# Forming the sums of the FFN's weights in DRAM by adding transfers

## The chip, the core and the metric

The kernel runs on one core of one Trainium2 chip. Its engines are TensorE (PE), VectorE (DVE), ScalarE (ACT) and GpSimd (POOL); SyncE (SP) issues transfers, and 16 DMA engines move them. Each engine takes its instructions in one fixed order. The metric is the device time of one execution in microseconds (us), the median of the runs.

## The reference

One decoder block on 1024 tokens of width 1024 in float32:

```
u    = rmsnorm(x, g1);  proj = u @ w_in          # queries, keys, values, mLSTM inputs, gates
ya   = sliding_window_attention(q, k, v, sinks) @ w_attn_branch      # 8 heads of 64, window 128
ym   = (rmsnorm(mlstm(...), gm) * sigmoid(mo)) @ w_mlstm_branch      # 4 heads, chunks of 128
x    = x + (sigmoid(ga) * ya + sigmoid(gm) * ym) @ w_out
f    = rmsnorm(x, g2)
x    = x + (silu(f @ w_ffn_gate) * (f @ w_ffn_up)) @ w_ffn_down      # inner width 2816
out  = rmsnorm(x, g3)
```

## The kernel before

Every float32 operand of a product is split into two parts, hi and lo, of a format that PE multiplies: ACT rounds hi, and DVE or POOL subtracts it for lo (`split`, line 71). A product is three matmuls, hi·hi, hi·lo and lo·hi. Weights come in blocks of 128 columns (`weights`, line 75).

The program has these stages. In the opening x and the first weights are loaded, and u is split. Since the norm of a token is a factor of its row, products with u start at once, and the factor 1/rms goes in when a bank of PSUM is emptied. That factor, `rstd1`, is made from sums of squares by a power on POOL (line 141); PE spreads it with an identity into rows (`rows_of`, line 146), ACT stores them as `Rt`, and DVE multiplies the queries with them as it empties the banks (line 229). Seven banks hold query products till then. Then come keys, values, the attention in 16 units (`attn_a`, `attn_b`, `attn_c`), in which POOL subtracts the lo part of each unit's queries (line 289) and scales the probabilities by 1/den (line 314), mixed with the convolution's projections, whose lo parts POOL makes as well; the mLSTM; the two branches' projections; and the output projection.

The FFN follows. It uses a product scheme with seven products in place of eight for a 2 by 2 arrangement of blocks (the indices 1 to 7 in `ORDER` and `DORD`). Four of the seven take a sum or difference of blocks of the weights x11, x12, x21, x22: 5 is x21 + x22, 6 is that + x11, 7 is x11 + x21, 3 is x12 + sum 6. Gate and up have 22 such sets of seven products (pair n, `product7`), 11 for gate and 11 for up. Before, SP loads the four blocks of a set (`load_pair`, line 791), and POOL forms the four sums in SBUF (line 813) ahead of the split (`prep`, line 805). The inner activations and their sums go to DRAM (`hd_`, `h_store`, line 867). Down reads them back by `dload` (line 959), with blocks of its weights, and POOL forms their sums (lines 987 to 995), with a copy on ACT for two of them, ahead of the split in `dprep`.

The program is written in one order and recorded; a scheduler then places each engine's instructions by its own estimate of when they can start. A written place is thus no fixed place: what depends on nothing can move to the front of its engine's order.

Of the kernel before, what the change touches and what calls it, by code (L numbers as in the profile page):

```python
# [15 lines left out]
P = 128  # L16
# [2 lines left out]
FF = 2816  # L19
KD = D // P  # L20
NF = FF // P
NT = S // P
HALF = 512
EPS = 1e-6
# [5 lines left out]


@with_exitstack
def hybrid_block(ctx, tc, xT, xt, par, g3row, cst, abias, w_fm, w_mv, w_br, w_o, w_gu, w_dn, out):
    nc = tc.nc
    V, A, G, T = nc.vector, nc.scalar, nc.gpsimd, nc.tensor

# [14 lines left out]
    def blk(name, dtype=F32, n=1024):  # L51
        return sb.tile([P, n], dtype, name=name, tag="blk", bufs=NB)
# [22 lines left out]
    def weights(src, nk, w=P):  # L75

        return weights_split(weights_load(src, nk * w), nk, w)
# [36 lines left out]
    def hs(h):  # L114
        return slice(h * HALF, (h + 1) * HALF)
# [517 lines left out]
    run(gai, 16)  # L633


    ph_a.close()
    lo_eng[0] = V
    ph_b = ExitStack()
# [22 lines left out]
            os_[h][p] = (pv2(hi), pv2(lo))  # L661
    o_ = lambda k, h: tuple(b[:, k % 2] for b in os_[h][k // 2])
    for j in range(KD):
        wt = weights(w_br[j], 4)
        A.activation(mg[j], mg[j], AF.Sigmoid)
        for h in range(2):
            ps = proj(wt, o_, 4, h)
            V.tensor_tensor(mg[j][:, hs(h)], ps, mg[j][:, hs(h)], ALU.mult)


    hs_ = [[None, None], [None, None]]
    for i in range(4):
# [14 lines left out]

    m = []
    for j in range(KD):
        wt = weights(w_fm[22 + j], KD)  # L690
# [12 lines left out]
        split(hi, lo, mg[j])  # L703
        m.append((hi, lo))
# [66 lines left out]
    def half(name, tag, bufs):  # L771
        return pC.tile([P, HALF], F32, name=name, tag=tag, bufs=bufs)
# [9 lines left out]


    ORDER = (1, 6, 5, 7, 2, 3, 4)
    NP2 = NF // 2
# [3 lines left out]
    raws, hl, sums = {}, {}, {}  # L789

    def load_pair(n):

        raws[n] = [x for i in range(2) for x in pair_raw(n, i)]

    def pair_raw(n, i):
        if n == 0 and i == 1:
            r = [half("wr", "ev", 6) for _ in range(2)]
            for k in range(2):
                nc.sync.dma_start(out=r[k], in_=w_gu[n, i, :, hs(k)])
            return r  # L800
        r = blk("wr2") if i else wp.tile([P, 1024], F32, name="wraw", tag="wraw", bufs=2)
        nc.sync.dma_start(out=r, in_=w_gu[n, i])
        return halves(r)

    def prep(g):
        n, i = SEQ[g]
        if n and i == 6 and n + 1 < 2 * NP2:
            load_pair(n + 1)
        x11, x12, x21, x22 = raws[n]

        def s_(k, a, b):
            sums[n, k] = half("s_", "ws", 5)
            G.tensor_tensor(sums[n, k], a, b, ALU.add)  # L813
        if i in (5, 6) and (n, 5) not in sums:
            s_(5, x21, x22)
        if i == 6:
            s_(6, sums[n, 5], x11)
        elif i == 7:
            s_(7, x11, x21)
        elif i == 3:  # L820
            s_(3, x12, sums[n, 6])
        src = {1: x11, 2: x12, 4: x22}
        hi = wp.tile([P, HALF], F32R, name="whi", tag="whi", bufs=5)
        lo = wp.tile([P, HALF], F32R, name="wlo", tag="wlo", bufs=5)
        split(hi, lo, src[i] if i in src else sums[n, i])
        hl[n, i] = (hi, lo)

    later = []
    for j in range(KD):
        wt = weights(w_o[j], KD)  # L830
        xr = wp.tile([P, 1024], F32, name="xr2", tag="wraw", bufs=2)
        nc.sync.dma_start(out=xr, in_=xT[j])
        xc = blk("xc")
        f = blk("f")
        F_.append(f)
        g = prm[:, C_G2 + j:C_G2 + j + 1]
        if j == KD - 1:
            load_pair(0)
            prep(0)
            prep(1)  # L840
        for h in range(2):
            ps = proj(wt, m_, KD, h)
            V.tensor_tensor(xc[:, hs(h)], ps, xr[:, hs(h)], ALU.add)
            A.activation(f[:, hs(h)], xc[:, hs(h)], AF.Copy, scale=g)
            later.append((xc, j, h))
            if len(later) > 1:
                to_tokens(*later.pop(0))
        if j % 2 == 1 and j < 6:
            f_even(j // 2)
        elif j == 6:  # L850
            f_split(1, 3, F_[6][:, 0:HALF])
# [81 lines left out]
            if i == 4 and s == 1:  # L933
                h_sums(n // 2, sg)

    load_pair(1)

    def f_rest(i, kt):
        (z11, z12), (z21, z22) = halves(F_[2 * kt]), halves(F_[2 * kt + 1])
# [9 lines left out]
    DORD = (1, 5, 2, 3, 6, 7, 4)  # L949
    NC_ = 7 * NP2  # L950
    LD, LP = 6, 4
    draw, dop, sT, dtm = {}, {}, {}, {}

    def t_at(p):
        if (p // 2) not in sT:
            sT[p // 2] = blk("sT")
        return halves(sT[p // 2])[p % 2]

    def dload(c):

        i, p = DORD[c // NP2], c % NP2
        t = blk("ld")
        draw[c] = t
        nc.sync.dma_start(out=t[:, 0:HALF], in_=hd_[i - 1, p])

        def ld(k, j, dst=None):
            dst = half("lz", "ev", 6) if dst is None else dst
            nc.sync.dma_start(out=dst, in_=w_dn[2 * p + k, :, hs(j)])
            return dst
        z = t[:, HALF:1024]  # L970
        if i in (1, 2, 3):
            ld(*{1: (0, 0), 2: (1, 0), 3: (1, 1)}[i], z)
        elif i == 5:
            dtm[c] = ld(0, 0), ld(0, 1)
        elif i == 7:
            dtm[c] = ld(1, 1), ld(0, 1)
        elif i == 6:
            dtm[c] = (ld(1, 1),)
        else:
            dtm[c] = (ld(1, 0),)  # L980

    def dprep(c):
        i, p = DORD[c // NP2], c % NP2
        t = draw.pop(c)
        z, tm = t[:, HALF:1024], dtm.pop(c, None)
        if i == 5:
            G.tensor_tensor(t_at(p), *tm, ALU.add)
            A.activation(z, t_at(p), AF.Copy)
        elif i == 6:
            G.tensor_tensor(t_at(p), tm[0], t_at(p), ALU.add)  # L990
            A.activation(z, t_at(p), AF.Copy)
        elif i == 7:
            G.tensor_tensor(z, *tm, ALU.add)
        elif i == 4:
            G.tensor_tensor(z, tm[0], t_at(p), ALU.add)
        hi, lo = blk("xzh", F32R), blk("xzl", F32R)
        split(hi, lo, t)
        dop[c] = hi, lo

    z11, z12 = halves(F_[6])  # L1000
# [2 lines left out]
        f_rest(6, kt)  # L1003
    prep(2)
    prep(3)
    rest = [(i, kt) for i in (7, 2, 3, 4) for kt in range(4)]
    for g, (n, i) in enumerate(SEQ):
        if g + LA < len(SEQ):
            prep(g + LA)
        product7(n, i)  # L1010
        if g == 0:
            to_tokens(*later.pop(0))
            V.tensor_tensor(rstd2, ss2[:, 0], ss2[:, 1], ALU.add)
            rstd_of(rstd2, rstd2, D, NT)
        if n == 2 * NP2 - 1 and i in (7, 2, 3):
            for c in {7: range(LP), 2: range(2), 3: range(2, LP)}[i]:
                (dload if i == 7 else dprep)(c)
        for _ in range(2):
            if rest:
                f_rest(*rest.pop(0))  # L1020
# [95 lines left out]
def _layout(i):  # L1116
# [30 lines left out]
    def cols(w):  # L1147
# [12 lines left out]
    w_br = np.concatenate([cols(wa), cols(a["w_mlstm_branch"][0])], axis=0)  # L1160
    w_o = cols(a["w_out"][0])

    w_gu = np.stack([cols(a[k][0]).reshape(NF // 2, 2, P, 4, 2, P).transpose(0, 1, 2, 4, 3, 5).reshape(NF // 2, 2, P, D)
                     for k in ("w_ffn_gate", "w_ffn_up")], axis=1).reshape(NF, 2, P, D)
    w_dn = a["w_ffn_down"][0].reshape(NF, P, D)
    return [xT, x.reshape(NT, P, D), par, np.tile(a["final_norm_g"][None, :], (P, 1)), cst, abias, w_fm, w_mv, w_br, w_o, w_gu, w_dn]


_NAMES = ["xT", "xt", "par", "g3row", "cst", "abias", "w_fm", "w_mv", "w_br", "w_o", "w_gu", "w_dn"]


# [15 lines left out]
```

## Time and profile before

| | us |
|---|---|
| median of 3 runs | 1335.22 (1332.36 to 1336.35) |
| the profiled execution | 1331.28 |
| its span, first to last instruction | 1329.5 |
| PE busy in the span | 1303.4 (98%) |
| DVE, ACT, POOL busy | 765.0, 572.7, 458.5 |
| moved by DMA | 143.13 MB, mean 108 GB/s |

The profiled execution is 1.8 us longer than its span and 3.9 us below the median. A busy time is the sum over an engine's instructions; matmuls overlap, so busy 98% means that PE hardly waits. The row of the granted clock in the page's slices is 9 (of tenths, 9 is 90% or more) in all but two of the 40 slices, where it is 8.

### The profile page before, as it was taken

Reading aid. Unit: us, or ns where it says so; the run is one execution under the profiler, and the core shown is the slowest. Engines: PE = TensorE matmul, PEld = TensorE weight load, DVE = VectorE, ACT = ScalarE, POOL = GpSimd, SP = SyncE. Lnnn points to the kernel's source line nnn. Section 1 sums busy time; section 2 is a strip of 40 time slices with the busy share of each in tenths; the row PEclk is TensorE's granted clock in tenths of the full one; section 3 lists DMA queues with packets and bytes.
Section 4 is the critical chain, followed back from the end, with each engine's and each line's share of the span. In section 5 each row is a group of like instructions: output and inputs, shape, how many; then the busy total and the mean of one; then the engine's idle time right before and its main releaser. Section 6 shows DMA issues by size and latency. Waiting matters only on the chain.

```text
span 1329.5 us, 16764 instructions
## 1 busy us (share of the span) xinstructions
PE 1303.4 (98%) x6090; PEld 1066.1 (80%) x6090; DVE 765.0 (58%) x1261; ACT 572.7 (43%) x1078; POOL 458.5 (34%) x374
## 2 busy tenths in 40 slices
PE   8999999999999999999989999999999999999986
PEld 6888998777888888888778888888888888888865
DVE  5369764565535444433587555555556564664796
ACT  6369974566213222224453333333233344565333
POOL 0245443211000000010266657556655725600470
PEclk9999999999999999999989999999999999999989
DMA  9111011101111111224323321323232249983761
GB/s 338 48 57 39 17 33 48 49 9 33 56 48 42 44 48 49 73 64 158 121 67 121 119 97 71 103 103 119 104 119 82 85 168 309 331 287 92 261 230 64
DMA packets 61860, 143.13 MB, mean 108 GB/s; under 512 B 6992, under 2 KB 7248, under 8 KB 61776
## 3 DMA queue, kind: packets, MB, share of 16 engines
q1 hardware_dynamic: 61776, 142.05, 31.7%
q8 instruction: 48, 0.79, 0.2%
q14 instruction: 36, 0.29, 0.1%
HBM read 113.45 MB, written 28.57 MB: 107 GB/s over the span
## 4 chain that ended last, share of the span: by engine, by line
PE 87%; DVE 7%; issue 2%; ACT 1%; DMA 1%; POOL 1%; SPq 0%; DVEq 0%; POOLq 0%; ACTq 0%
PE mm L108 8%; PE mm L110 7%; PE mm L109 7%; PE mm L856 6%; PE mm L857 6%; PE mm L855 6%; PE mb L856 5%; PE mb L857 5%; PE mb L855 5%; PE st L857 4%; PE st L855 4%; PE st L856 4%; PE mb L110 4%; PE mb L109 4%; PE mb L108 4%
## 5 line engine op out<-in xcount | busy, mean ns | idle before, releaser
L72 ACT ACTIVATE whi<-wraw 128x512 fp32r<-128x512 f32 (+1 forms) x144 | 89.3, 628 | 221.3 <-PE mb L109 99.8
L73 DVE TENSOR_TENSOR xzl<-ld,xzh 128x1024 fp32r<-128x1024 f32 x77 | 110.4, 1463 | 69.3 <-ACT xzh L72 62.0
L108 PE MATMUL mm<-uh,whi 128*128 128x512 f32 x352 | 140.0, 400 | 1.1 <-ACT whi L72 1.1
L110 PE MATMUL mm<-uh,wlo 128*128 128x512 f32 x352 | 139.0, 395 | 0.0
L109 PE MATMUL mm<-ul,whi 128*128 128x512 f32 x352 | 138.7, 395 | 0.0
L73 DVE TENSOR_TENSOR wlo<-wraw,whi 128x512 fp32r<-128x512 f32 (+1 forms) x116 | 88.6, 771 | 76.4 <-ACT whi L72 75.5
L72 ACT ACTIVATE xzh<-ld 128x1024 fp32r<-128x1024 f32 x77 | 79.7, 1056 | 58.5 <-DMA ld<-in_w_dn_dram 24.9
L857 PE MATMUL mb<-z,wlo 128*128 128x512 f32 x220 | 87.8, 399 | 1.8 <-DVE wlo L73 1.8
L856 PE MATMUL mb<-z,whi 128*128 128x512 f32 x220 | 87.7, 399 | 0.0
L855 PE MATMUL mb<-z,whi 128*128 128x512 f32 x220 | 87.7, 399 | 0.0
L855 PE MATMUL mm<-z,whi 128*128 128x512 f32 x220 | 86.7, 394 | 0.0
L857 PE MATMUL mm<-z,wlo 128*128 128x512 f32 x220 | 86.7, 394 | 0.0
L856 PE MATMUL mm<-z,whi 128*128 128x512 f32 x220 | 86.7, 394 | 0.0
L813 POOL TENSOR_TENSOR s__5671<-wr 128x512 f32<-128x512 f32 x1 | 1.5, 1538 | 232.9 <-DMA wr<-in_w_gu_dram 232.9
L108 PEld LDWEIGHTS mm<-uh,whi 128*128 128x128 f32 x352 | 66.3, 188 | 17.0 <-ACT whi L72 2.3
L921 POOL TENSOR_TENSOR w<-w,d 128x512 f32<-128x512 f32 x22 | 36.0, 1636 | 126.7 <-DVE w L920 122.9
L110 PEld LDWEIGHTS mm<-uh,wlo 128*128 128x128 f32 x352 | 66.2, 188 | 15.6 <-DVE wlo L73 0.2
L109 PEld LDWEIGHTS mm<-ul,whi 128*128 128x128 f32 x352 | 66.3, 188 | 14.4
L857 PE MATMUL st<-z,wlo 128*128 128x512 f32 x176 | 69.4, 394 | 0.0
L855 PE MATMUL st<-z,whi 128*128 128x512 f32 x176 | 69.4, 394 | 0.0
L856 PE MATMUL st<-z,whi 128*128 128x512 f32 x176 | 69.2, 393 | 0.0
L890 ACT ACTIVATE sg<-sg 128x512 f32<-128x512 f32 x44 | 27.7, 629 | 88.1 <-DVE sg L889 49.9
(591 smaller groups left out, 3431.1 us busy)
## 6 DMA issues: line engine op xcount, KB each, us to landing
ld<-hd__5018 SPq DMA_DIRECT2D x77, 256.0 KB, 4.7
lz<-in_w_dn_dram SPq DMA_DIRECT2D x66, 256.0 KB, 4.9
wraw<-in_w_fm_dram SPq DMA_DIRECT2D x28, 512.0 KB, 3.5
wraw<-in_w_gu_dram SPq DMA_DIRECT2D x22, 512.0 KB, 3.6
hd__5018<-hs SPq DMA_DIRECT2D x44, 256.0 KB, 2.1
wr<-in_w_gu_dram SPq DMA_DIRECT2D x21, 512.0 KB, 6.0
hd__5018<-sg SPq DMA_DIRECT2D x33, 256.0 KB, 2.3
ld<-in_w_dn_dram SPq DMA_DIRECT2D x33, 256.0 KB, 5.2
```

The costliest lines, as they stand in the source:

```text
L72: A.activation(hi, src, AF.Copy)
L73: eng.tensor_tensor(lo, src, hi.bitcast(F32), ALU.subtract)
L108: T.matmul(ps, ah, bh, start=(i == 0), stop=False)
L109: T.matmul(ps, ah, bl, start=False, stop=False)
L110: T.matmul(ps, al, bh, start=False, stop=(i == n - 1))
L813: G.tensor_tensor(sums[n, k], a, b, ALU.add)
L855: T.matmul(ps, xh, zh, start=start, stop=False, skip_group_check=more)
L856: T.matmul(ps, xh, zl, start=False, stop=False, skip_group_check=more)
L857: T.matmul(ps, xl, zh, start=False, stop=stop, skip_group_check=more)
L890: A.activation(dst, dst, AF.Silu)
L921: G.tensor_tensor(e["w"], e["w"], e["d5"], ALU.subtract)
```

## The change

The weights of gate and up, and of down, lie in DRAM as four arrays of blocks each (`wx`, `wd`). Eight arrays in DRAM, wS0 to wS3 and wT0 to wT3, take the sums. A generator, `add_up`, forms them: POOL issues a copy of one array, then a transfer that adds another array to it, for two arrays at first, then for a sum of sums, and so on. In gate and up each array goes in two parts; every transfer has 352 rows of 2048 float32. The program calls the generator between the weights of the branches, and the one of down after sets of gate and up. Gate and up then load the operand of each product by itself, 256 KB, from wx or wS, four products ahead of the split (`load`); down loads from wd or wT. The sums on POOL and the copies on ACT are gone.

```diff
+    wS = [dr.tile([NF * 32, 2048], F32, name=f"wS{k}") for k in range(4)]
+    wT = [dr.tile([NP2 * 32, 2048], F32, name=f"wT{k}") for k in range(4)]
+    def add_up(x, s, groups):
+        x11, x12, x21, x22 = x
+        for steps in (((0, x21, 0), (2, x11, 0)), ((0, x22, 1), (2, x21, 1)), ((1, s[0], 0),), ((1, x11, 1),),
+                      ((3, s[1], 0),), ((3, x12, 1),)):
+            for k, src, add in steps:
+                for r in groups:
+                    if add:
+                        G.dma_start(out=s[k][r], in_=src[r], accum_op=ALU.add, max_dma_last_dim=8192)
+                    else:
+                        G.dma_start(out=s[k][r], in_=src[r], max_dma_last_dim=8192)
+                    yield
+    ffn_sums = add_up([wx[b] for b in range(4)], wS, [slice(0, NP2 * 32), slice(NP2 * 32, NF * 32)])
+    down_sums = add_up([wd[b] for b in (3, 2, 1, 0)], wT, [slice(0, NP2 * 32)])
...
     for j in range(KD):
+        run(ffn_sums)
         wt = weights(w_br[j], 4)
...
+    raw_of = {1: wx[0], 2: wx[1], 4: wx[3], 5: wS[0], 6: wS[1], 7: wS[2], 3: wS[3]}
+    def load(g):
+        if g < len(SEQ):
+            n, i = SEQ[g]
+            raws[g] = half("wo", "wo", 5)
+            nc.sync.dma_start(out=raws[g], in_=wblock(raw_of[i], n))
...
     def prep(g):
...
-        if i in (5, 6) and (n, 5) not in sums:
-            s_(5, x21, x22)
-        if i == 6:
-            s_(6, sums[n, 5], x11)
-        elif i == 7:
-            s_(7, x11, x21)
-        elif i == 3:
-            s_(3, x12, sums[n, 6])
...
     def dprep(c):
...
-        if i == 5:
-            G.tensor_tensor(t_at(p), *tm, ALU.add)
-            A.activation(z, t_at(p), AF.Copy)
...
     for g, (n, i) in enumerate(SEQ):
+        load(g + LA + LL)
         if g + LA < len(SEQ):
             prep(g + LA)
         product7(n, i)
+        if i == 4 and n < 10:
+            run(down_sums)
```

The order of POOL, opening of the program, before: the power that makes `rstd1` is the first work, and the attention's queries (`qs`) follow.

```order
L141 ISA
L141 TENSOR_TENSOR rstd1_92<-rstd1_92,nhalf_85 128x8
L289 TENSOR_TENSOR qs_621<-qT_414,qs_621 64x256
L289 TENSOR_TENSOR qs_715<-qT_414,qs_715 64x256
L289 TENSOR_TENSOR qs_621<-qT_415,qs_621 64x256
```

The same place now (L650 is a copy, L648 a transfer that adds; x2 are the two parts):

```order
L650 DMA wS0_3561<-in_w_x_dram 352x2048 x2
L650 DMA wS2_3563<-in_w_x_dram 352x2048 x2
L648 DMA wS0_3561<-in_w_x_dram 352x2048 x2
L648 DMA wS2_3563<-in_w_x_dram 352x2048 x2
L650 DMA wS1_3562<-wS0_3561 352x2048 x2
L648 DMA wS1_3562<-in_w_x_dram 352x2048 x2
L142 ISA
L142 TENSOR_TENSOR rstd1_92<-rstd1_92,nhalf_85 128x8
L650 DMA wS3_3564<-wS1_3562 352x2048 x2
L290 TENSOR_TENSOR qs_621<-qT_414,qs_621 64x256
L290 TENSOR_TENSOR qs_715<-qT_414,qs_715 64x256
```

Twelve transfers have come ahead of the power. POOL, a little further, before: lo parts of the convolution's weights (`wlo`), queries of the third to fifth unit, and the scaling of the first unit's probabilities (`s`).

```order
L73 TENSOR_TENSOR wlo_837<-wraw_830,whi_836 128x512
L73 TENSOR_TENSOR wlo_1022<-wraw_1019,whi_1021 128x512
L289 TENSOR_TENSOR qs_795<-qT_414,qs_795 64x256
L289 TENSOR_TENSOR qs_795<-qT_415,qs_795 64x256
L314 TENSOR_SCALAR s_619<-s_619,den_644 128x128 x4
L289 TENSOR_TENSOR qs_891<-qT_414,qs_891 64x256
L289 TENSOR_TENSOR qs_891<-qT_415,qs_891 64x256
L289 TENSOR_TENSOR qs_984<-qT_414,qs_984 64x256
```

The same place now:

```order
L74 TENSOR_TENSOR wlo_837<-wraw_830,whi_836 128x512
L650 DMA wT1_3566<-wT0_3565 352x2048
L74 TENSOR_TENSOR wlo_1022<-wraw_1019,whi_1021 128x512
L290 TENSOR_TENSOR qs_795<-qT_414,qs_795 64x256
L290 TENSOR_TENSOR qs_795<-qT_415,qs_795 64x256
L648 DMA wT1_3566<-in_w_d_dram 352x2048
L650 DMA wT3_3568<-wT1_3566 352x2048
L315 TENSOR_SCALAR s_619<-s_619,den_644 128x128 x4
L290 TENSOR_TENSOR qs_891<-qT_414,qs_891 64x256
L290 TENSOR_TENSOR qs_891<-qT_415,qs_891 64x256
L648 DMA wT3_3568<-in_w_d_dram 352x2048
L290 TENSOR_TENSOR qs_984<-qT_414,qs_984 64x256
```

The last of the 24 transfers stands ahead of the fifth unit's queries; none is left for the branches or for gate and up. On PE one thing has moved, the matmuls that spread `rstd1`. Before:

```order
L108 MATMUL tp<-uh,whi 128x512
L109 MATMUL tp<-ul,whi 128x512
L110 MATMUL tp<-uh,wlo 128x512
L146 MATMUL po<-idn,rstd_92 128x128 x4
L108 MATMUL tp<-uh,whi 128x512
```

Now, where `tp` is the seventh half product of the queries, and `mm` the eighth:

```order
L109 MATMUL tp<-uh,whi 128x512
L110 MATMUL tp<-ul,whi 128x512
L111 MATMUL tp<-uh,wlo 128x512
L147 MATMUL po<-idn,rstd_92 128x128 x8
L109 MATMUL mm<-uh,whi 128x512
```

They stand behind all seven half products instead of among the last of them.

## Rows read from the trace of the kernel before

**Rows 1.** Page, part 1: busy us (share of the span), instructions.
```profile
PE 1303.4 (98%) x6090; PEld 1066.1 (80%) x6090; DVE 765.0 (58%) x1261; ACT 572.7 (43%) x1078; POOL 458.5 (34%) x374
```
**Rows 2.** Page, part 4: the chain that ended last, by engine.
```profile
PE 87%; DVE 7%; issue 2%; ACT 1%; DMA 1%; POOL 1%; SPq 0%; DVEq 0%; POOLq 0%; ACTq 0%
```
**Rows 3.** Stretches of the FFN: us, busy by engine, granted clock, DMA share, GB/s.
```profile
core 0: us, PE busy (x) PEld busy (x) DVE busy (x) ACT busy (x) POOL busy (x), PEclk, DMA share, GB/s
640.00:1000.00 360.00, 354.73 (x1532) 287.13 (x1531) 225.01 (x285) 130.62 (x232) 216.74 (x143) 0.99 0.31 104
1000.00:1290.00 290.00, 286.11 (x1223) 231.22 (x1222) 178.39 (x171) 126.26 (x172) 125.49 (x83) 0.99 0.62 211
1290.00:1329.00 39.00, 28.41 (x122) 22.45 (x120) 27.14 (x36) 11.47 (x22) 5.31 (x6) 0.95 0.15 55
```
**Rows 4.** PE's waits, 560 to 1290 us: us in total, times, longest.
```profile
PE mb L856 <- DVE xzl L73: 3.9, 2, 3.1
PE mm L146 <- DVE v L916: 3.4, 1, 3.4
PE mb L857 <- DVE wlo L73: 1.8, 1, 1.8
```
**Rows 5.** Stretches of the opening, columns as in rows 3.
```profile
0.00:33.20 33.20, 29.72 (x117) 22.95 (x118) 19.75 (x30) 20.38 (x28) 0.19 (x4) 1.00 0.92 338
...
10.00:25.00 15.00, 15.00 (x66) 12.16 (x65) 10.76 (x11) 9.04 (x10) 0.00 (x0) 1.00 1.03 406
33.20:91.00 57.80, 57.80 (x276) 47.65 (x275) 24.08 (x57) 25.63 (x58) 17.30 (x18) 1.00 0.17 55
```
**Rows 6.** POOL in order of time, 0 to 110 us: start, us, instruction, idle before.
```profile
34.59 1.66 POOL L141 TENSOR_TENSOR rstd<-rstd,nhalf 128x8 f32<-128x8 f32 x1 [34.17 <-DVE rstd L140]
44.15 1.55 POOL L289 TENSOR_TENSOR qs<-qT,qs 64x256 fp32r<-64x256 f32 x2 [7.89 <-ACT qs L288]
49.85 1.54 POOL L289 TENSOR_TENSOR qs<-qT,qs 64x256 fp32r<-64x256 f32 x2 [4.15 <-ACT qs L288]
54.72 1.29 POOL L73 TENSOR_TENSOR wlo<-wraw,whi 128x512 fp32r<-128x512 f32 x1 [3.33 <-ACT whi L72]
...
84.83 3.24 POOL L314 TENSOR_SCALAR s<-s,den 128x128 f32<-128x128 f32 x4 [3.72 <-DVE den L312]
88.16 1.44 POOL L289 TENSOR_TENSOR qs<-qT,qs 64x256 fp32r<-64x256 f32 x2
92.26 1.53 POOL L289 TENSOR_TENSOR qs<-qT,qs 64x256 fp32r<-64x256 f32 x2 [2.67 <-ACT qs L288]
```
**Rows 7.** PE in order of time: spreading, last of the seven, first scores.
```profile
39.66 1.05 PE L146 MATMUL po<-idn,rstd 128*128 128x128 f32 x8
...
46.80 0.40 PE L110 MATMUL tp<-uh,wlo 128*128 128x512 f32 x1
...
76.61 0.31 PE L295 MATMUL sc<-kh,qs 128*128 128x128 f32 x1
```
**Rows 8.** Waits in SP's queue, whole run: us in total, times, longest.
```profile
SPq L81 <- DVE wlo L73: 269.2, 32, 32.8
SPq L81 <- POOL wlo L73: 209.4, 14, 31.2
...
SPq L869 <- POOL sg L892: 116.9, 11, 11.9
```
**Rows 9.** Page, part 6: transfers issued, KB each, median us to landing.
```profile
ld<-hd__5018 SPq DMA_DIRECT2D x77, 256.0 KB, 4.7
...
hd__5018<-hs SPq DMA_DIRECT2D x44, 256.0 KB, 2.1
```
**Rows 10.** POOL's sums: line 813 by stretch; line 987, ns min/median/max.
```profile
640.00:1000.00 360.00, 114.78 (x74) 0.99 0.31 104
1000.00:1290.00 290.00, 20.34 (x14) 0.99 0.62 211
...
L987 POOL TENSOR_TENSOR sT<-lz x11: 1282/1302/2269, 1113.0 to 1140.1; 128x512 f32<-128x512 f32 x11
```

More of the change, by code (lines that the diff above doesn't have):

```diff
@@ L21 @@
 NF = FF // P
+NP2 = NF // 2
 NT = S // P
@@ L32, in hybrid_block @@
 @with_exitstack
-def hybrid_block(ctx, tc, xT, xt, par, g3row, cst, abias, w_fm, w_mv, w_br, w_o, w_gu, w_dn, out):
+def hybrid_block(ctx, tc, xT, xt, par, g3row, cst, abias, w_fm, w_mv, w_br, w_o, wx, wd, out):
     nc = tc.nc
@@ L672, in hybrid_block @@
     for i in range(4):
+        run(ffn_sums, 2)
         wt = weights(w_fm[18 + i], KD)
@@ L689, in hybrid_block @@
     for j in range(KD):
+        run(ffn_sums)
         wt = weights(w_fm[22 + j], KD)
@@ L784, in hybrid_block @@
     ORDER = (1, 6, 5, 7, 2, 3, 4)
-    NP2 = NF // 2
     SEQ = [(n, i) for i2 in ((1, 5), (6, 7), (2, 3, 4)) for n in range(2) for i in i2]
@@ L788, in hybrid_block, with wblock @@
     LA = 4
[L789 to L803, printed above, removed]
-    def prep(g):
[L806 to L813, printed above, removed]
-        if i in (5, 6) and (n, 5) not in sums:
-            s_(5, x21, x22)
-        if i == 6:
-            s_(6, sums[n, 5], x11)
-        elif i == 7:
-            s_(7, x11, x21)
-        elif i == 3:
-            s_(3, x12, sums[n, 6])
-        src = {1: x11, 2: x12, 4: x22}
+    raws, hl = {}, {}
+    LL = 4
+    def wblock(w, n):
+        return w[n * 32:(n + 1) * 32].rearrange("r (b c) -> (r b) c", c=HALF)
+    raw_of = {1: wx[0], 2: wx[1], 4: wx[3], 5: wS[0], 6: wS[1], 7: wS[2], 3: wS[3]}
[4 more added lines that the diff above has]
+            nc.sync.dma_start(out=raws[g], in_=wblock(raw_of[i], n))
+    def prep(g):
         hi = wp.tile([P, HALF], F32R, name="whi", tag="whi", bufs=5)
         lo = wp.tile([P, HALF], F32R, name="wlo", tag="wlo", bufs=5)
-        split(hi, lo, src[i] if i in src else sums[n, i])
-        hl[n, i] = (hi, lo)
+        split(hi, lo, raws.pop(g))
+        hl[SEQ[g]] = (hi, lo)
     later = []
@@ L837, in hybrid_block @@
         if j == KD - 1:
-            load_pair(0)
+            for g_ in range(LL):
+                load(g_)
             prep(0)
@@ L934, in product7 @@
                 h_sums(n // 2, sg)
-    load_pair(1)
+    for g in range(LL, 7):
+        load(g)
     def f_rest(i, kt):
@@ L951, in hybrid_block @@
     LD, LP = 6, 4
[L952 to L957, printed above, removed]
+    draw, dop = {}, {}
+    z_of = {1: wd[0], 2: wd[2], 3: wd[3], 5: wT[0], 6: wT[1], 7: wT[2], 4: wT[3]}
     def dload(c):
         i, p = DORD[c // NP2], c % NP2
-        t = blk("ld")
-        draw[c] = t
+        draw[c] = t = blk("ld")
         nc.sync.dma_start(out=t[:, 0:HALF], in_=hd_[i - 1, p])
[L966 to L980, printed above, removed]
-    def dprep(c):
-        i, p = DORD[c // NP2], c % NP2
-        t = draw.pop(c)
-        z, tm = t[:, HALF:1024], dtm.pop(c, None)
-        if i == 5:
-            G.tensor_tensor(t_at(p), *tm, ALU.add)
-            A.activation(z, t_at(p), AF.Copy)
[L989 to L995, printed above, removed]
+        nc.sync.dma_start(out=t[:, HALF:1024], in_=wblock(z_of[i], p))
+    def dprep(c):
         hi, lo = blk("xzh", F32R), blk("xzl", F32R)
-        split(hi, lo, t)
+        split(hi, lo, draw.pop(c))
         dop[c] = hi, lo
@@ L1005, in hybrid_block @@
     prep(3)
+    load(7)
     rest = [(i, kt) for i in (7, 2, 3, 4) for kt in range(4)]
     for g, (n, i) in enumerate(SEQ):
+        load(g + LA + LL)
         if g + LA < len(SEQ):
@@ L1161, in _layout @@
     w_o = cols(a["w_out"][0])
[L1163 to L1169, printed above, removed]
+    w_x = np.stack([cols(a[k][0]).reshape(NP2, 2, P, 4, 2, P).transpose(1, 4, 0, 2, 3, 5).reshape(4, NP2, P, HALF)
+                    for k in ("w_ffn_gate", "w_ffn_up")], axis=2).reshape(4, NF * 32, 2048)
+    w_d = np.ascontiguousarray(a["w_ffn_down"][0].reshape(NP2, 2, P, 2, HALF).transpose(1, 3, 0, 2, 4)).reshape(4, NP2 * 32, 2048)
+    return [xT, x.reshape(NT, P, D), par, np.tile(a["final_norm_g"][None, :], (P, 1)), cst, abias, w_fm, w_mv, w_br, w_o, w_x, w_d]
+_NAMES = ["xT", "xt", "par", "g3row", "cst", "abias", "w_fm", "w_mv", "w_br", "w_o", "w_x", "w_d"]
 def kernel(**inputs):
```

## The prediction

> **What bounds the kernel now.** I read the page's busy table first: PE is busy 1303.4 of 1329.5 us, 98% of the span; POOL 458.5 [rows 1]. The chain that ended last is PE for 87% [rows 2]. Then I cut the span into stages: in gate and up (640 to 1000 us) PE is idle 360 − 354.73 = 5.3 us, in down (1000 to 1290) 290 − 286.11 = 3.9 us, and only the last 39 us have a gap of 10.6 us, which the change does not touch [rows 3]. What PE waits for between 560 and 1290 is operands split late, 3.9 and 1.8 us, and once 3.4 us for the second norm [rows 4]. So the stage that the change means to relieve has some 9 us to give. The reader should therefore look at the other end of the program, where the new transfers stand.
>
> In the opening the DMA engines are full: 0 to 33.2 us moves 338 GB/s at a busy share of 0.92, and 10 to 25 us 406 GB/s at 1.03; behind that, to 91 us, only 55 GB/s [rows 5]. All PE work behind seven half products hangs on the first norm: POOL makes its power at 34.59 us, in its first work of any length [rows 6]; PE spreads it into rows at 39.66 us, and DVE can empty no query bank without them. PE ends the seven half products at about 47 us, and needs the first queries, split on POOL from 44.15 us, at 76.61 us [rows 6, 7].
>
> **What the change removes.** POOL's sums of gate and up, 88 of them, 114.78 + 20.34 = 135 us [rows 10], and 44 in down, of which one line of eleven has a median of 1.30 us [rows 10]; and 22 copies on ACT. PE loses no matmul. Since PE waits only 9 us in both stages, this removes between 0 and 9 us of the time; I take 4. The loads added are 7 blocks of 256 KB for each set of seven products, 7 × 22 × 262 KB = 40 MB over some 430 us, with engines that stand at a share of 0.31 in gate and up [rows 3]. They queue on SP behind stores that wait up to 11.9 us for POOL [rows 8]. They are hidden by the depth ahead: four loaded and four prepared products, each twelve matmuls of 360 us / 1532 = 0.235 us, so 8 × 2.8 = 22 us. Without that cover the eleven long waits would cost up to 11 × 11.9 = 131 us; I take nothing, because POOL, on which those stores wait, loses 135 us of work.
>
> **What it adds, and where.** There are 24 transfers of 352 × 2048 × 4 = 2.884 MB from DRAM to DRAM, 12 copies and 12 that add to what is there; 69 MB in all. In the source they stand behind the branches. In POOL's instruction order they stand in front: twelve of them ahead of the power of the first norm, and the other twelve between it and the queries of the fifth attention unit. Each that reads or adds to an earlier one's result waits for that one to land, and POOL goes on only when it has. The trace shows a queue held in this way on SP: its issues wait 269.2 us for wlo of DVE and 209.4 us for that of POOL, and those behind wait with them [rows 8]. So every piece of POOL work listed behind a transfer waits for the transfers ahead of it, and PE behind that.
>
> The price is bytes over a rate that the trace does not show, since it has no transfer within DRAM and none that adds. Bounds for a copy: at best it runs as the full loads do, 406 GB/s [rows 5]; at worst as one 256 KB store to DRAM that lands in 2.1 us, 125 GB/s [rows 9]. A transfer that adds reads twice, so I halve both: 203 down to 62 GB/s. I take 406 as the engines' rate for one pass through DRAM: a copy makes two passes, 203 GB/s; an addition three, 135 GB/s. These lie between the bounds, nearer to the row of full engines, since 2.9 MB is long against a landing time. The Trainium skill, "DMA: Bandwidth & Descriptors", section on latency and other measured facts, gives 207 to 214 GB/s in each direction for copies between HBM tensors; no row here shows it. By it the copies below would take 162 us and not 170, an estimate.
>
> - Opening loads: 33.2 us × 338 GB/s = 11.2 MB, and 57.8 × 55 = 3.2 MB to 91 us [rows 5]; 14.4 MB / 406 = 35 us of the same engines.
> - Until the power: 6 copies (17.3 MB, 85 us) and 4 additions (11.5 MB, 85 us) must have landed, since the two additions right ahead of it wait for the last of them and are then only issued; and 28 us for the first 11.2 MB: about 198 us in place of 34.59. PE, at its spreading matmuls at about 47 us of its work, stands some 150 us.
> - Until the queries of the fifth unit (92.26 us before [rows 6]): 12 copies, 34.6 MB / 203 = 170 us; 11 additions (the twelfth is only issued), 31.7 MB / 135 = 235 us; loads 35 us. Most transfers have another queued behind them; three at the end (the copy and addition to the second sum of down, the copy to its last) do not. For these I add 3 × 5 us, from the loaded landing time of 4.7 [rows 9], and 20 us for the places where POOL waits in between for ACT and DVE (gaps of 3 to 8 us in the same stretch before [rows 6]). Sum: 170 + 235 + 35 + 35 = 475 us.
>
> Before, POOL stands at this place at about 91 us. PE's 45 us of work between the power and here runs beside the transfers, so it is in the sum already. If PE's clock were at its lower level when it starts again, this is also hidden there: all stretches of the opening show 1.00, and the last stage, with PE busy 28 of 39 us, 0.95 [rows 3, 5]. Delay: 475 − 91 = 384 us; what follows runs as before. Sum against the profiled execution: 1331.3 + 384 − 4 = 1711 us. The median shown is 1335.22, 3.9 above that execution, so the forecast is 1715.
>
> **The rivals.**
> (A) The transfers run at the best bounds, because eight-kilobyte rows keep all engines busy in both directions at once: copies at 406, additions at 203: 85 + 156 + 35 + 35 = 311, a delay of 220, and 1331 + 220 − 4 = 1547 us. With additions at 406 too: 233, so 1469. For it: 10 to 25 us shows the engines full at 406. Against: that is one pass through DRAM, not two or three. The Trainium skill, same page, section on the anatomy of a DMA of the gpsimd path, fits 2.0 us + bytes / 436 GB/s, without a distinction by where the data lies. That would be 8.6 us a transfer, 198 us for 23, and with my 70 us around them an estimate of about 1504 us.
> (B) Additions at the slow bound, since each row must be read from two places, summed and written back without overlap: 31.7 MB / 62.5 = 507 us; 170 + 507 + 70 = 747, a delay of 656, 1983 us. Nothing in the trace speaks against it; for it only a store's landing time [rows 9], which is mostly latency.
> (C) Not slower: POOL does not stand at a waiting transfer but passes on to its work, and the new copies get only what the loads leave. Then the power comes at 34.59 as before, all sums end long before gate and up, and the time is 1331 − 4 to 1331 − 9, about 1325 us. It decides from the point at which the first norm is on time. Against it: SP's held queue [rows 8], and that POOL's compute shows the same strict order before, where the power waits 34 us at the head and nothing passes it [rows 6].
> (D) As (C), but the copies of the opening share the engines with the loads: 11.2 MB at half of 406 takes 28 us more, 1331 + 28 − 4 = 1355 us.
>
> **How the numbers follow.** My forecast has 0.70, with a range of its own from 1630 (its 405 us of transfers take a fifth less) to 1873 (40% more). (A) 0.12, (B) 0.12, (C) 0.03, (D) 0.03. The range reaches from (A)'s upper case to just under (B): 1540 to 1960 us. About 0.3% (4 us) is what a measurement of this kernel tells from no change. Faster comes from (C) alone, 0.02, within 0.3% from the rest of it, 0.01; slower 0.97.
>
> **What would show it.** In the profile after: POOL's power at 150 to 260 us, and PE's spreading matmuls waiting for it more than 100 us, the longest wait of the run; slices 2 to 14 with POOL and PE mostly idle, and DMA full; a new software queue of 69 MB; the granted clock under 1 there; and from some 475 us on the same work as before from 91 us. In the later stages PE's idle time goes down by a few us, no more. The forecast is wrong if the power comes before 60 us, or if PE waits longer in gate and up than its 5 us, or if the sums have all landed before some 300 us and the run still is longer than (A)'s.

## The result, and the profile after

The kernel became slower: 1557.15 us (1556.0 to 1557.93) beside 1334.88 (1332.36 to 1336.35) for the kernel before on the same chip, a ratio of 1.1667 with an interval of 1.1647 to 1.1687. That is 222 us more; the forecast was 380 more. The direction and the place were right, the size was not.

The page of the kernel after, parts 1, 2 and 4, answers to [rows 1, 2]. In part 2 each character is one of 40 slices of 38.9 us.

```profile
PE 1321.9 (85%) x6090; PEld 1077.2 (69%) x6090; DVE 702.3 (45%) x1261; ACT 561.4 (36%) x1056; POOL 271.5 (17%) x266
...
PE   5800631259999999999999999999999999999997
...
POOL 0000111135431110000000032333333333200010
PEclk9955775569999999999999999999999999999999
DMA  9988888882001001111122435444444445766561
...
PE 73%; issue 18%; DMA 3%; DVE 2%; POOL 2%; ACT 1%; POOLq 0%; DVEq 0%; ACTq 0%
```

PE does the same 6090 matmuls, and POOL is relieved of 187 us. But in slices 2 to 8 (78 to 350 us) PE is mostly idle, its clock row shows 5 to 7 of tenths, where 5 is the lower of its two levels (1.2 GHz), and the DMA engines are nearly full. The chain has 18% of "issue" where it had 2%: an engine that waits for nothing that has a name in the profile.

The stretches of the kernel after answer to [rows 3, 5]; columns as there. The last three rows are single transfers: an addition, a copy, an addition.

```profile
core 0: us, PE busy (x) PEld busy (x) DVE busy (x) ACT busy (x) POOL busy (x), PEclk, DMA share, GB/s
0.00:33.20 33.20, 15.42 (x31) 9.05 (x31) 5.58 (x13) 7.51 (x10) 2.77 (x8) 1.00 0.93 337
33.20:91.00 57.80, 38.49 (x144) 29.51 (x144) 15.88 (x20) 13.45 (x19) 1.98 (x2) 0.87 1.02 306
91.00:315.00 224.00, 53.01 (x208) 42.60 (x208) 22.64 (x54) 25.60 (x60) 25.38 (x28) 0.61 0.86 211
...
865.00:1225.00 360.00, 359.52 (x1576) 291.21 (x1575) 197.99 (x290) 135.44 (x239) 106.55 (x70) 1.00 0.44 139
1225.00:1515.00 290.00, 290.00 (x1255) 235.28 (x1254) 154.39 (x176) 117.83 (x159) 40.60 (x28) 1.00 0.61 208
...
110.20:127.20 17.00, 0.00 (x0) 0.00 (x0) 0.00 (x0) 0.00 (x0) 0.90 (x1) 0.50 0.86 170
...
296.95:307.75 10.80, 8.39 (x32) 6.81 (x32) 7.73 (x27) 9.15 (x28) 2.73 (x3) 0.82 0.81 267
307.75:324.72 16.97, 0.00 (x0) 0.00 (x0) 0.00 (x0) 0.00 (x0) 0.93 (x2) 0.50 0.86 170
```

An addition of 2.884 MB takes 17.0 us (170 GB/s), a copy 10.8 us (267 GB/s). In the FFN PE has almost no gap left: 359.5 of 360 us and 290.0 of 290, at a clock of 1.00.

POOL in order of time answers to [rows 6] (start, us, instruction, idle before it and what ended it). L650 is a copy, L648 an addition.

```profile
47.23 1.02 POOL L648 DMA_DIRECT2D wS<-in_w_x_dram  x1 [21.37 <-issue]
70.22 0.96 POOL L648 DMA_DIRECT2D wS<-in_w_x_dram  x1 [21.96 <-issue]
92.14 0.94 POOL L648 DMA_DIRECT2D wS<-in_w_x_dram  x1 [20.97 <-issue]
110.17 0.93 POOL L648 DMA_DIRECT2D wS<-in_w_x_dram  x1 [17.09 <-issue]
127.20 1.20 POOL L650 DMA_DIRECT2D wS<-wS  x2 [16.11 <-issue]
147.46 0.97 POOL L648 DMA_DIRECT2D wS<-in_w_x_dram  x1 [19.06 <-issue]
164.73 0.95 POOL L648 DMA_DIRECT2D wS<-in_w_x_dram  x1 [16.30 <-issue]
165.45 2.06 POOL L142 TENSOR_TENSOR rstd<-rstd,nhalf 128x8 f32<-128x8 f32 x1
...
307.75 0.93 POOL L648 DMA_DIRECT2D wT<-in_w_d_dram  x1 [7.99 <-DMA wT<-wT]
324.72 0.61 POOL L650 DMA_DIRECT2D wT<-wT  x1 [16.03 <-DMA wT<-in_w_d_dram]
...
336.07 1.05 POOL L648 DMA_DIRECT2D wT<-in_w_d_dram  x1 [7.73 <-DMA wT<-wT]
337.18 1.86 POOL L290 TENSOR_TENSOR qs<-qT,qs 64x256 fp32r<-64x256 f32 x2
```

The power comes at 165.45 us instead of 34.59, the fifth unit's queries at 337.18 instead of 92.26: 244.9 us later. From 91 to 315 us POOL works for 25 us, the issuing of transfers included; the rest is standing.

The waits of PE in the kernel after, whole run, longest first (us in total, times, longest):

```profile
PE po L147 <- POOL rstd L142: 90.5, 1, 90.5
PE sc L296 <- DVE mx L300: 44.8, 1, 44.8
PE mm L111 <- POOL wlo L74: 28.7, 1, 28.7
PE tp L330 <- POOL s L315: 24.3, 2, 20.5
```

Only the second names another engine than POOL, and it comes from POOL too. DVE stood 42.9 of those 44.8 us for the load of `ab`, which SP issued at 279.65 us instead of 75.9, since SP's queue was held by a block whose lo part POOL had not made. The two rows are of SP, in its waits from 30 to 345 us and in its timeline:

```profile
SPq L82 <- POOL wlo L74: 162.7, 3, 61.6
```

```profile
279.65 0.48 SPq L269 DMA_DIRECT2D ab<-in_abias_dram  x1
```

Three marks on PE show where the time stays: at the last scores of the mLSTM, at the first product of gate and up, and at the last matmul of down. Before:

```profile
315.43 0.71 PE L540 MATMUL sc<-qk 64*128 64x128 f32 x8
...
657.30 0.48 PE L855 MATMUL mm<-z,whi 128*128 128x512 f32 x1
...
1320.26 0.39 PE L857 MATMUL st<-xzh,xzl 128*128 128x512 f32 x1
```

After:

```profile
559.92 0.71 PE L541 MATMUL sc<-qk 64*128 64x128 f32 x8
...
901.79 0.48 PE L860 MATMUL mm<-z,whi 128*128 128x512 f32 x1
...
1546.84 0.39 PE L862 MATMUL st<-xzh,xzl 128*128 128x512 f32 x1
```

The first two are each 244.5 us later, the last 226.6. So the whole loss arises ahead of the first mark, where it agrees with POOL's delay of 244.9 us, and the FFN gives back 17.9 us. 244.5 − 17.9 = 226.6, the difference of the two spans (1556.1 − 1329.5).

### The profile page after: what moved, and what is told of

The parts are those of the page before. It is cut to its first block, busy times and chain, and to the rows that moved or that the text cites. A ratio compares the mean times of both kernels' runs of the same rounds, so it can differ in the third digit from the quotient of the medians.

```text
span 1556.1 us, 16805 instructions
## 1 busy us (share of the span) xinstructions
PE 1321.9 (85%) x6090; PEld 1077.2 (69%) x6090; DVE 702.3 (45%) x1261; ACT 561.4 (36%) x1056; POOL 271.5 (17%) x266
## 4 chain that ended last, share of the span: by engine, by line
PE 73%; issue 18%; DMA 3%; DVE 2%; POOL 2%; ACT 1%; POOLq 0%; DVEq 0%; ACTq 0%
PE mm L109 5%; PE mm L111 5%; PE mm L110 5%; PE mm L861 5%; PE mm L860 5%; PE mm L862 5%; PE mb L860 5%; PE mb L862 5%; PE mb L861 5%; PE st L860 4%; PE st L861 4%; PE st L862 4%; PE mb L111 3%; PE mb L110 3%; PE mb L109 3%
## 5 line engine op out<-in xcount | busy, mean ns | idle before, releaser
L111 PE MATMUL mm<-uh,wlo 128*128 128x512 f32 x352 | 143.8, 408 | 28.7 <-POOL wlo L74 28.7
L73 ACT ACTIVATE whi<-wo 128x512 fp32r<-128x512 f32 x154 | 96.9, 629 | 194.0 <-PE st L861 59.8
L109 PE MATMUL mm<-uh,whi 128*128 128x512 f32 x352 | 146.6, 419 | 20.7 <-ACT uh L184 14.9
L73 ACT ACTIVATE whi<-wraw 128x512 fp32r<-128x512 f32 (+1 forms) x100 | 61.6, 628 | 228.8 <-PE mb L110 99.8
L110 PE MATMUL mm<-ul,whi 128*128 128x512 f32 x352 | 143.8, 409 | 0.0
L74 DVE TENSOR_TENSOR wlo<-wo,whi 128x512 fp32r<-128x512 f32 x154 | 113.3, 735 | 63.9 <-ACT whi L73 63.9
L74 DVE TENSOR_TENSOR xzl<-ld,xzh 128x1024 fp32r<-128x1024 f32 x77 | 92.7, 1244 | 79.6 <-ACT xzh L73 70.3
L109 PEld LDWEIGHTS mm<-uh,whi 128*128 128x128 f32 x352 | 69.7, 199 | 41.0 <-ACT uh L184 19.2
L147 PE MATMUL po<-idn,rstd 128*128 128x128 f32 x16 | 4.1, 441 | 91.2 <-POOL rstd L142 90.5
L74 DVE TENSOR_TENSOR wlo<-wraw,whi 128x512 fp32r<-128x512 f32 (+1 forms) x72 | 48.8, 690 | 62.2 <-ACT whi L73 62.2
```

The costliest lines, as they stand in the source:

```text
L73: A.activation(hi, src, AF.Copy)
L74: eng.tensor_tensor(lo, src, hi.bitcast(F32), ALU.subtract)
L109: T.matmul(ps, ah, bh, start=(i == 0), stop=False)
L110: T.matmul(ps, ah, bl, start=False, stop=False)
L111: T.matmul(ps, al, bh, start=False, stop=(i == n - 1))
L147: T.matmul(ps[:, t * P:(t + 1) * P], rs[:, c0 + t:c0 + t + 1].to_broadcast([P, P]), idn, start=True, stop=True)
```

## The experiments

The theory was: POOL stands at transfers that came ahead of its work, and this alone costs the time. The rivals were that the load of the transfers on the DMA engines costs it, that the wait for the power alone does, and that the FFN's new loads matter. Times of the kernel before are 1334.9 to 1336.3 us in all the comparisons below.

**No transfers.** The places that issue transfers go, and gate, up and down load stored blocks where sums were.

```diff
-        run(ffn_sums)
...
-    raw_of = {1: wx[0], 2: wx[1], 4: wx[3], 5: wS[0], 6: wS[1], 7: wS[2], 3: wS[3]}
+    raw_of = {1: wx[0], 2: wx[1], 4: wx[3], 5: wx[2], 6: wx[1], 7: wx[0], 3: wx[3]}
...
-    z_of = {1: wd[0], 2: wd[2], 3: wd[3], 5: wT[0], 6: wT[1], 7: wT[2], 4: wT[3]}
+    z_of = {1: wd[0], 2: wd[2], 3: wd[3], 5: wd[1], 6: wd[0], 7: wd[2], 4: wd[3]}
...
-            run(down_sums)
```

> All 24 transfers are left out, and gate, up and down load a stored block in the place of each sum (so the output is not the reference's); all else is as in the changed kernel. This is the gain of the FFN alone. If the gain of 18 us seen from the start of gate and up to the end of the changed run comes from PE no longer waiting for split operands: 1331 - 18 = 1313 us, PE waiting less than 1 us in gate and up. If instead part of it is only a side effect of the late start (a loaded memory, another clock), the time is the forecast's 1327 us. The opening is then as before, with the power of the first norm at 34.6 us.

Measured: 1315.95 us, 0.9845 (0.9828 to 0.9861). The part of the change in the FFN is a gain of 20 us, and the new loads cost nothing: PE waits 0.5 us in gate, up and down together. The weights of gate and up are now 40 MB of loads, 154 blocks of 256 KB. Before they were 23 MB (43 loads of 512 KB, 2 of 256), so 17 MB were added. All the loss, and more, comes from the transfers.

**The transfers behind the mLSTM.** Each transfer is told to come behind the last power issued so far, and keeps the written order among the others.

```diff
+    powers = []
...
     def rstd_of(dst, ss, n, nt):
...
-        G.tensor_tensor(dst[:, :nt], dst[:, :nt], nhalf[:, :nt], ALU.pow)
+        powers.append(G.tensor_tensor(dst[:, :nt], dst[:, :nt], nhalf[:, :nt], ALU.pow))
...
+                    with tc.issue_after(powers[-1].ins):
+                        how = dict(accum_op=ALU.add) if add else {}
+                        tc.keep_in_program_order(G.dma_start(out=s[k][r], in_=src[r], max_dma_last_dim=8192, **how))
```

> Same transfers and same sums, but each is held in its written place in POOL's order, behind the last power of the mLSTM; the eight of down stay in gate and up, one behind a set. If POOL's order is the cause, the first norm is on time, the sixteen of gate and up take 8 x 10.8 + 8 x 17.2 = 224 us from about 320 us on, while POOL has nothing else, and the eight of down hold POOL by up to 17 us each beside gate and up: 1313 us if this is covered, up to 1313 + 8 x 17 = 1449 if it is not. If the transfers cost by loading the DMA engines and the memory, wherever they stand, the time stays near 1557 - 28 = 1529.

Measured: 1326.45 us, 0.9928 (0.9913 to 0.9943). The same 24 transfers, 69 MB, now cost 10.5 us over the run without them. Those of gate and up are issued from 334.63 to 555.41 us, where POOL has almost nothing else to do. PE in that stretch, and its longest wait in the FFN:

```profile
316.00:560.00 244.00, 243.44 (x1086) 197.50 (x1085) 109.83 (x185) 70.80 (x126) 15.61 (x19) 1.00 0.85 226
```

```profile
PE mb L861 <- ACT v L920: 6.1, 3, 2.2
```

PE is busy 243.44 of 244 us beside DMA engines at 0.85 and 226 GB/s: their load does not slow PE here. The run without transfers has 243.43 us in the same stretch, at 47 GB/s. The 10.5 us left are in gate and up, where down's eight transfers stand 14 to 31 us apart: PE is idle there for 6.1 us, and the rest goes to slower matmuls behind each wait. POOL stands up to 11.9 us at these transfers, but PE's row names ACT's `v` and not POOL. Ahead of `v` in its order ACT stood for loads from wS (660 to 900 us; in total, times, longest):

```profile
ACT whi L73 <- DMA wo<-wS: 49.9, 9, 10.4
```

Beside down's transfers the loads of gate and up took up to 18.7 us to land, and at most 4.5 in the run without transfers, where ACT waits for none of them. So the trace puts the 10 us down to late loads. That POOL's standing adds to them is not shown.

**Copies only.** Every addition becomes a copy, in the same places; the sums are then left out.

```diff
-                        G.dma_start(out=s[k][r], in_=src[r], accum_op=ALU.add, max_dma_last_dim=8192)
+                        G.dma_start(out=s[k][r], in_=src[r], max_dma_last_dim=8192)
```

> Each adding transfer is a plain copy of the same bytes in the same place (the sums are not formed, so the output is not the reference's). If an addition costs 17.2 us and a copy 10.8, eleven of them ahead of the fifth unit's queries save 11 x 6.4 = 70 us: 1557 - 70 = 1487, and POOL is free at 337 - 70 = 267 us. If each transfer costs what its wait for the one before costs, and not its kind, the time stays at 1557.

Measured: 1458.97 us, 1.0921 (1.0899 to 1.0943), 98 us less than with additions. The fifth unit's queries come at 237.46 instead of 337.18 us, 99.7 less: the run follows POOL's place almost one to one.

```profile
237.46 1.77 POOL L290 TENSOR_TENSOR qs<-qT,qs 64x256 fp32r<-64x256 f32 x2
```

The expected 70 us was (17.2 − 10.8) times 11 additions. Of the 30 us that it missed, 22 arise up to the end of the first four additions, at 127.20 us, where this run is at 79.56. Ahead of the first of them POOL stands until 47.23 us instead of 37.09, and the four take 17 to 23 us each, the first three beside the opening's loads, while the copies in their place are 9 to 11 us apart. Since an addition also needs more room in POOL's queue than a copy (next experiment), this run changes the rate and the room together, and does not price the rate alone.

**More room for transfers on POOL's queue.** The memory for descriptors that POOL writes goes from 1024 to 4096 bytes of each partition, one buffer of 4 KB less in turn.

```diff
-    NB, NB2, NX = 37, 5, 1032
+    NB, NB2, NX = 36, 5, 1032
...
-    nc = _bacc.Bacc("TRN2", target_bir_lowering=False, num_devices=1, dynamic_dma_scratch_size=1024)
+    nc = _bacc.Bacc("TRN2", target_bir_lowering=False, num_devices=1, dynamic_dma_scratch_size=4096)
```

> The changed kernel with four times the room for descriptors of POOL's transfers (4096 bytes a partition in place of 1024; one buffer of 4 KB less for it). In the changed run POOL stands 15 to 22 us ahead of each transfer with no semaphore as the cause, and the second of a pair of additions is issued only when the first has run (147.5 and 164.7 us). If that is missing room and the sum of transfer times sets the end: POOL issues the second addition at once, the power comes at about 148 us in place of 165.4, the copies overlap a little better, and the run is within 15 us of 1557, since every transfer still waits for its data. If room is what holds POOL, the transfers overlap, the fifth unit's queries come 50 us or more earlier, and the run is at 1500 or below.

Measured: 1516.52 us, 1.1357 (1.1336 to 1.1377), 41 us less, between the two expectations. The power comes at 135.27 us, and the fifth unit's queries at 295.29 us, 42 us earlier. POOL's timeline shows what changed:

```profile
1.26 2.57 POOL L650 DMA_DIRECT2D wS<-in_w_x_dram  x4 [0.82 <-POOLq L1154]
15.66 1.00 POOL L648 DMA_DIRECT2D wS<-in_w_x_dram  x1 [11.84 <-DMA wS<-in_w_x_dram]
...
64.92 0.60 POOL L650 DMA_DIRECT2D wS<-wS  x1 [16.34 <-DMA wS<-in_w_x_dram]
```

Four copies go out at once instead of two, and where the kernel after shows "issue" there is now a landing. So "issue" ahead of a transfer on POOL was a queue without room, and this standing cost 41 us of the 222, some 1.8 us for each of 23 transfers. The larger part stays: POOL now stands for the landing of earlier transfers in the same places, as the rows name it.

**The power first.** All transfers are told to come behind the first power, and are not tied otherwise.

```diff
+        powers.append(G.tensor_tensor(dst[:, :nt], dst[:, :nt], nhalf[:, :nt], ALU.pow))
...
+                    with tc.issue_after(powers[0].ins):
+                        how = dict(accum_op=ALU.add) if add else {}
+                        G.dma_start(out=s[k][r], in_=src[r], max_dma_last_dim=8192, **how)
```

> Only the power of the first norm is put ahead of all transfers; the rest may move as the scheduler likes, and they stay among the attention's POOL work. PE's longest wait, 90.5 us for that power, must go. If the first wait were the cost, the run is 90 us shorter, 1467 us. If the last place where POOL stands decides: the chain starts at 36 us and not at 1, takes about 24 x 14.3 = 343 us, ends at about 380 us between attention units that POOL reached at about 125 us before, a delay of 255 in place of 244, so 1557 to 1570 us.

Measured: 1543.38 us, 1.1558 (1.1537 to 1.1579). The power runs at 36.74 us and the longest wait of PE, 90.5 us, is gone; yet the run is only 14 us shorter. That is far from the first expectation, and 14 us under the range of the second, which put the end of the chain at 380 us. PE's waits of this kernel:

```profile
PE tp L332 <- POOL s L317: 124.5, 9, 31.0
PE sc L298 <- DVE mx L302: 37.0, 1, 37.0
```

The lost time turned into waits for POOL's next work. The last transfer is issued at 362.29 us, and what stands among and behind the transfers sets the end, not the wait that was the longest.

**POOL freed.** Additions behind the first power; down's transfers pinned in gate and up; POOL's part of the attention and of the lo parts there goes to DVE. The transfers stay beside the attention.

```diff
-            G.tensor_tensor(qs[rest, d], src, qs[rows, d].bitcast(F32), ALU.subtract)
+            V.tensor_tensor(qs[rest, d], src, qs[rows, d].bitcast(F32), ALU.subtract)
...
-            G.tensor_scalar(sv[:, hh, c0:256], sv[:, hh, c0:256], den[:, hh:hh + 1], 1.0, ALU.mult, ALU.mult)
+            V.tensor_scalar(sv[:, hh, c0:256], sv[:, hh, c0:256], den[:, hh:hh + 1], 1.0, ALU.mult, ALU.mult)
...
-    lo_eng[0] = G
+    lo_eng[0] = V
...
+                    if s is wT:
+                        with tc.issue_after(powers[-1].ins):
...
+                    elif add:
+                        with tc.issue_after(powers[0].ins):
+                            G.dma_start(out=s[k][r], in_=src[r], accum_op=ALU.add, max_dma_last_dim=8192)
```

> The first four copies stay at the front and the twelve other transfers of gate and up follow the power of the first norm at once; the attention's POOL work (the lo parts of queries and weights, the scaling by 1/den) goes to DVE, so nothing is queued behind these transfers until the mLSTM; down's eight are held in gate and up. If POOL's standing is the cost: 1313, plus 30 to 60 us for an opening whose loads share the engines with copies, plus up to 40 us for the DVE work added: 1345 to 1415. If the shared DMA engines are the cost, sixteen of 24 transfers still run there: 1313 + 244 x 224 / 337 = 1475.

Measured: 1369.13 us, 1.0248 (1.0228 to 1.0269). The transfers of gate and up are issued from 1.25 to 245 us (1.25 to 221 with the change), and POOL stands at them as before, but nobody waits behind it. One stretch of this kernel:

```profile
91.00:245.00 154.00, 143.54 (x859) 126.38 (x858) 121.76 (x406) 111.28 (x269) 7.29 (x10) 0.96 0.88 218
```

PE is busy 143.5 of 154 us beside engines at 0.88. The span is 54.6 us over that of the run without transfers. Of these 29 arise before the attention's first scores (108.2 us instead of 79.0), where the copies share the engines with the opening's loads; the power comes at 66.52 us. Another 17 arise by the end of the attention (270.4 instead of 224.1). That second part can be DVE's added work or the transfers' load on the DMA engines; this run does not separate them. Some 2 us are made up after it, and 11 are lost in gate and up, where down's eight transfers stand as in the second experiment.

**Down's transfers moved as well.** As the second experiment, but four of down's transfers right behind those of gate and up, and four behind gate and up.

```diff
+    run(down_sums, 4)
     x2d = dr.tile([NT, P, D], F32, name="x2d")
...
-        if i == 4 and n < 10:
-            run(down_sums)
...
+    run(down_sums, 4)
+
     def dmm(ps, c, t, start, stop, more):
```

> As the kernel held behind the mLSTM, with down's eight transfers out of gate and up: four right behind those of gate and up, four behind gate and up. If the 10 us between that run (1326.45) and the one without transfers (1315.95) are POOL standing beside gate and up: 1316 to 1320 us, and PE's waits for v, 6.1 us, are gone. The four in front end at about 573 + 58 = 631 us and hold POOL's sums of f by up to 45 us; if that is not covered, up to 1326 + 10. If the 10 us come from the transfers' load on the DMA engines, they come back with the move: 1326.

Measured: 1363.64 us, 1.0206 (1.0192 to 1.022), a miss. PE now has no such waits in gate and up, but they start 36.7 us later than in the second experiment, and down waits for its last sums (PE busy 204.62 of 213 us there). POOL's order:

```profile
615.59 0.96 POOL L651 DMA_DIRECT2D wT<-in_w_d_dram  x1 [16.42 <-issue]
616.23 1.61 POOL L794 TENSOR_TENSOR f<-f 128x512 f32<-128x512 f32 x1
```

The sums of the FFN's input stand behind the fourth transfer, at 616 us instead of 585. DVE waits 34.0 us for what they feed, and PE 27.0 for DVE. POOL's free stretch had been filled to the end; four more transfers ran over it.

**Down's transfers spaced out.** As the second experiment, with one transfer of down behind every second set of products.

```diff
-        if i == 4 and n < 10:
+        if i == 4 and n % 2 == 0 and n < 16:
             run(down_sums)
```

> As the kernel held behind the mLSTM (1326.45), but down's eight transfers stand behind every second set of gate and up, some 39 us apart, instead of behind each. Each then finds its data landed and room in the queue. If the 10 us to the run without transfers are POOL standing up to 12 us at a transfer beside gate and up: no standing there, PE's 6.1 us of waits for v gone, and 1316 to 1319 us. If they come from the transfers' load on the DMA engines during gate and up: 1326 again, since the bytes are the same.

Measured: 1314.39 us, 0.9847 (0.9834 to 0.9861): 1.5% faster than before, faster than every other kernel here that forms the sums, and like the run without transfers (0.9845). The first and the last of down's transfers on POOL, PE's stretch in gate and up, and ACT's wait for loads (660 to 980 us):

```profile
672.77 0.69 POOL L651 DMA_DIRECT2D wT<-in_w_d_dram  x1
...
948.41 0.95 POOL L651 DMA_DIRECT2D wT<-in_w_d_dram  x1
```

```profile
657.00:1090.00 433.00, 432.52 (x1878) 350.15 (x1877) 239.48 (x342) 161.01 (x276) 140.39 (x97) 1.00 0.68 202
```

```profile
ACT whi L73 <- DMA wo<-wS: 19.3, 4, 5.1
```

The transfers are 39 to 42 us apart, each has landed when the next is issued, and POOL does not stand at one of down's eight; PE's 6.1 us of waits for `v` are gone. ACT still waits for loads, but at most 5.1 us, and none of it reaches PE. The time is the one expected of POOL's standing, but the run took away both, that standing and the long waits for loads, and does not separate them; ACT's rows speak for the loads. So the same 24 transfers and the same bytes cost nothing in this order and 243 us in the order of the change.

## Why the prediction was right, and where its size was wrong

**The order and the mechanism: right, and shown.** POOL stands at each transfer, its work behind them comes late, and PE behind that. With the same transfers in other places the loss is gone (1326.45, 1314.39); with POOL's work taken away from behind them most of it is (1369.13). Rivals (C) and (D) needed POOL to pass on; the power at 165 us excludes them. Rival (B) needed additions at 62 GB/s; they ran at 168 to 170. The DMA engines' load has a price of its own beside the opening's loads, 29 us in the run with POOL freed. In the change it lies inside POOL's standing, since the delay at the first mark, 244.5 us, is POOL's 244.9.

**The place that sets the end: right; its time was mis-sized.** The measured 1557 us is inside the stated range, 1540 to 1960, only because that range was stretched down to rival (A); the forecast's own range began at 1630. The forecast named the fifth unit's queries and put them at 475 us; they came at 337. The 138 us between have three parts, counted with the single transfers shown above:

| term | forecast | by single transfers measured |
|---|---|---|
| 12 copies | 170 us (203 GB/s) | 12 × 10.8 = 130 us (267 GB/s) |
| 11 additions | 235 us (135 GB/s) | 11 × 17.2 = 189 us (168 GB/s) |
| opening's loads, landings, POOL's other waits | 70 us | 337 − 319 = 18 us |

The first two failed in the step "406 as the engines' rate for one pass through DRAM: a copy makes two passes". A copy moves its bytes at 267 GB/s, two thirds of the 406 and not half, and an addition at 168 and not 135. The three passes of an addition stay an assumption: the profile counts 69 MB read and 69 MB written more for the 24 transfers (and 12 MB read for loads), and the same where all 24 are copies, so it shows no second read of the 12 that add. The third failed because its parts were added one behind the other. The opening's loads ran beside the transfers, and showed as some 5 us more in each of two additions (47 to 92 us); POOL's own work lay in its standing. Counted from issue to issue as they ran, the 12 copies took 132 us and the 11 additions 203, together 335 of the 337 us.

Rival (A)'s 1547 us, 10 from the result, was not right term by term: its transfers take 241 us where 319 were measured, and its 70 us around them are the same that turned out as 18. The two errors largely cancel, and that is luck. With the measured rates and those 70 us the sum would have been 389 − 91 = 298 us of delay. The Trainium skill, "DMA: Bandwidth & Descriptors", section on latency and other measured facts, gives 207 to 214 GB/s in each direction for copies between HBM tensors, on the queues of SP and ACT, in rows of 16 KiB and at two of the row pitches that it lists. This case's copy, from POOL's queue in rows of 8 KiB, ran at 267, and the measurement decides. The Trainium skill, same page, section on the anatomy of a DMA of the gpsimd path, fits 2.0 us + bytes / 436 GB/s to one transfer. That gives an estimate of 8.6 us, which is under both the 10.8 and the 17.2 measured.

**PE's wait for the power: right in kind, 90.5 instead of some 150 us.** The power came at 165 and not 198 us, 33 of the difference. The rest is PE: it ended its seven half products at some 77 us and not 47, since the opening's loads were slower (15.42 us of work in the first 33 instead of 29.72), so it had less left to wait. This cost to PE's own work stood under (D) only. The mark "more than 100 us" was missed for that reason, and it made little difference to the end: with the power first the whole wait is gone, and the run is 14 us shorter.

**What the forecast did not name.** SP's load of `ab` held by POOL, 44.8 us of PE's waits, and POOL's stand for room in its queue. The first is part of the same delay, and not added to it; the second cost 41 us. The 40 MB that the prediction calls added are all the loads of weights in gate and up, of which 17 MB are new; this did not enter the sum.

**The FFN: a gain of 18 to 20 us, forecast 4 of at most 9.** The step "PE waits only 9 us in both stages, this removes between 0 and 9" failed twice. It left the last 39 us out, where one of the removed waits, 2.2 us, stands. And it counted idle time alone, while the clock also falls after the waits. From the start of gate and up to the end of down PE was idle for 11.4 us before and for 0.5 after; the other 7 of the 18 us are slower matmuls. Two stretches of the kernel before, at the start of gate and up and late in down:

```profile
657.00:700.00 43.00, 37.73 (x161) 30.46 (x160) 38.65 (x50) 24.31 (x48) 27.11 (x17) 0.92 0.29 98
...
1270.00:1290.00 20.00, 19.05 (x70) 15.30 (x71) 18.88 (x13) 7.42 (x7) 15.97 (x9) 0.83 0.88 307
```

```profile
1270.95 0.79 PE L856 MATMUL mb<-xzl,xzh 128*128 128x512 f32 x1 [3.08 <-DVE xzl L73]
1271.54 0.63 PE L857 MATMUL mb<-xzh,xzl 128*128 128x512 f32 x1
1271.97 0.63 PE L855 MATMUL mb<-xzh 128*128 128x512 f32 x1
```

Behind this gap of 3.1 us the matmuls of the kernel before are 0.43 us apart instead of 0.23, and the granted clock of those 20 us is 0.83. After, the same stretches have 1.00. From the first product of gate and up to its last, and on to the last of down, gate and up went from 439.5 to 431.4 us and down from 223.4 to 213.6.

## What to carry to other kernels

When instructions of an in-order engine are moved, look for the last piece of work behind them that someone needs: its delay was the price here, and to remove the longest wait ahead of it moved most of the time to the next. A transfer that adds to what an earlier one writes is a wait on the engine that issues it. Give each a place where the one before has landed, or where that engine has nothing else to do, and check with the trace that such an idle stretch is as long as all the transfers in it together. Look at the loads beside the transfer as well, since they land later. And count the gain of a removed wait with the clock that falls behind it, not by the idle time alone.

## What the runs showed of the hardware

A copy within DRAM of 2.884 MB took 10.8 us (267 GB/s) and a transfer that adds to DRAM 17.0 to 17.2 us (168 to 170 GB/s), or 18 to 23 us beside the opening's loads. Beside such transfers a load of 256 KB in gate and up took up to 18.7 us to land, and at most 4.5 without them. With 1024 bytes of each partition for descriptors POOL stood until a transfer ahead had made room in its queue, with one addition or two copies in it; with 4096 four copies went out at once. DMA engines at a share of 0.85, moving 226 GB/s, most of it within DRAM, did not slow PE in the stretch of 244 us behind the mLSTM: 243.4 us busy, clock 1.00. With PE idle the granted clock was 0.50, at 110 to 127 us of the kernel after.
